# Two-layer hybrid encoder on one core: cast order in the down product, one reordered tile, postponed reciprocals, a last product in token halves

## Chip, cores and metric

One core of one Trainium2 chip runs the whole kernel in one launch. The metric is device time in microseconds (us), from the first to the last instruction with what lies around them; lower is better.

## The reference, cut to what matters

Input and output are 1024 tokens by 1024 channels in float32, and there are two layers. Layer 0 mixes tokens with a gated MLP over blocks of 128 tokens; layer 1 is attention over chunks of 64 tokens, each of which sees itself and the 8 chunks before it, with 16 heads of 64 channels and a clipped relative-position bias. Both layers end in a gated feed-forward block with a causal convolution of width 3, and a final RMSNorm closes.

```python
def conv_ffn(h, w_in, conv_w, conv_b, w_down):      # D_FF = 2816
    a = h @ w_in
    ...  # depthwise causal convolution of width 3, plus conv_b
    up, gate = jnp.split(a, 2, axis=-1)
    return (jax.nn.silu(gate) * up) @ w_down

# layer 0
h = h + gmlp_mixer(rmsnorm(h, a_norm_g[0]), ...)
h = h + conv_ffn(rmsnorm(h, f_norm_g[0]), ...)
# layer 1: keys and values come from the residual stream once
kv = rmsnorm(h, kv_norm_g) @ w_kv
h = h + chunk_attention(rmsnorm(h, b_norm_g[0]), k, v, ...)
h = h + conv_ffn(rmsnorm(h, f_norm_g[1]), ...)
return rmsnorm(h, final_norm_g)
```

## The kernel before

The residual stream h lies transposed, as 8 tiles of 128 channels by 1024 tokens; the two halves of 512 tokens are called t = 0 and t = 1. A float32 product is made of three matmuls in a faster format: each operand is split into a high part, the cast of itself by ScalarE, and a low part, the subtraction of that cast by VectorE (`split`, L135 to L138). High times high, low times high and high times low go into one PSUM bank.

**Order of the work.** TensorE's instructions run in the order in which the program writes them. On the other engines and queues a planner sets the order at build time from its own estimate of when an instruction's inputs are ready; each engine then runs its list strictly in order. `tc.issue_after(ins)` keeps what is issued inside it behind `ins` if both are on the same engine. `put_off(us, fn)` issues `fn` once the matmuls issued since add up to so many us of the program's own clock, so it also sets where `fn`'s matmuls stand in TensorE's list.

**Feed-forward, up side** (`ffn`, L636). Up and gate are computed by a Strassen scheme in 7 products, numbered 1 to 7, per tile of 128 of the 2816 features (`NF` = 22 tiles). A product is 12 matmuls of 512 columns. Products share PSUM: product 6 leaves a sum in one half of the gate bank, ScalarE copies it out (`keep`, L693), and product 7 goes on accumulating in that same half; product 3 goes on in the half where product 5 left its own. Tiles 0 and 1 are computed plainly, tile 2 is the first with 7 products, and the list `steps` (L658) writes the order out. After product 3 come the convolution of the up part, after product 4 that of the gate part and then SiLU (`conv`, `gated`). POOL makes the sums of blocks for the next stage and SyncE's queue stores them.

**Feed-forward, down side** (`down`, L779). Again 7 products, in the order 1, 6, 2, 7, 5, 4, 3, each over 11 steps: 77 steps a layer. A step takes a block d and a block g, splits them into w and x, and feeds 12 matmuls (3 for each of 4 output tiles m). Loads bring two steps at once (a set: one d tile and one g tile); sets take turns in two pools, two sets of every four from `new_raw`, two from `dx`. The w tiles have 4 places, the x tiles 16 that they share with others. `make` (L803) prepares steps up to four ahead. Up to step 23 the order on ScalarE, VectorE and SyncE is the program's own (`entry`); from step 24 on it is the planner's. When a product's 11 steps are done, `whole` (L815) adds its bank to h: product 7 adds into two tiles of h for each m, on POOL. In layer 1 the last four steps are taken together, output tile by output tile, so that the first tiles can be finished while the last are computed. When a half of the tokens is complete, `rstd_rows` sums the squares over channels by matmuls against ones (L229) and the norm follows (`norm` in layer 0, `final` in layer 1).

**Attention.** Heads go in pairs, each head in 8 blocks of keys. TensorE interleaves scores, values, the maxima of the next head (`Max`, L1054 and L1061, read by VectorE at L1057 and L1063), and the projections of the next pair. At the end of each half of the tokens a pair divides its outputs: `piece` (L1161) takes the reciprocal of the denominators in four pieces and multiplies; the fourth splits the result and stores it (`osave`). `stage` (L945) copies a head's keys and queries into place by DMA.

## Time and profile before

| | before |
|---|---|
| median of 3 runs | 2217.21 us (2214.3 to 2220.84) |
| the profiled execution | 2217.12 us |
| its span, first to last instruction | 2215.3 us |
| mean granted TensorE clock | 0.993 |
| TensorE matmul busy | 2152.2 us |

The times of the rows below are from that one profiled execution, counted from the start of its span. The mean granted clock is 1 at 2.4 GHz and 0.5 at 1.2 GHz.

### The profile page before, as it was taken

How to read it: one execution, taken by the hardware profiler on the slowest of the kernel's cores; microseconds unless marked ns; L12 is line 12 of the kernel's file. 1: busy time of each engine (PE TensorE's matmuls, PEld its weight loads, DVE VectorE, ACT ScalarE, POOL GpSimd, SP SyncE). 2: the span in 40 equal slices, each digit the busy share in tenths (PEclk: the TensorE clock that was granted, in tenths of full speed). 3: DMA queues.
4: the chain of work that ended last, by engine and by line, in shares of the span. 5: the costliest groups of instructions: out<-in, count | busy, mean ns of one | idle time of the engine just before them, and what ended most of it. 6: DMA issues, size and time to landing. Idle time of an engine off the chain costs nothing.

```text
span 2215.3 us, 28221 instructions
## 1 busy us (share of the span) xinstructions
PE 2152.2 (97%) x9880; PEld 1781.0 (80%) x9880; DVE 1584.9 (72%) x2418; ACT 1083.0 (49%) x1909; POOL 686.0 (31%) x471
## 2 busy tenths in 40 slices
PE   8999999999999999999999999999999999999998
PEld 7888887888888887768888888777778888888876
DVE  4763878988888665565776776654988888885555
ACT  6544445445444543445555555552544444454433
POOL 0301314423334112044444444351343334241020
PEclk9999999999999999999999999999999999999999
DMA  5242233445445865435444444644244444477652
GB/s 205 86 141 78 86 105 137 164 143 174 147 165 200 306 216 191 166 110 124 124 108 117 110 119 124 185 164 156 76 171 161 158 157 164 140 245 284 216 182 105
DMA packets 151534, 344.04 MB, mean 155 GB/s; under 512 B 31840, under 2 KB 32224, under 8 KB 151392
## 3 DMA queue, kind: packets, MB, share of 16 engines
q1 hardware_dynamic: 148080, 336.26, 46.7%
q10 hardware_dynamic: 3312, 5.98, 0.7%
q8 instruction: 77, 1.26, 0.2%
q14 instruction: 65, 0.53, 0.1%
HBM read 225.20 MB, written 87.56 MB: 141 GB/s over the span
## 4 chain that ended last, share of the span: by engine, by line
PE 48%; DVE 20%; issue 13%; DMA 11%; ACT 4%; POOL 2%; SPq 1%; POOLq 0%; DVEq 0%; ACTq 0%
DVE wlo L138 6%; DMA raw<-gT 5%; PE vps L465 4%; PE up L354 4%; PE up L356 4%; PE up L359 4%; PE gate L354 3%; PE gate L356 3%; PE gate L359 3%; DMA raw<-in_f_win 3%; DVE yl L138 2%; PE qkv L186 2%; PE qkv L182 2%; PE qkv L179 2%; DVE a L704 2%
## 5 line engine op out<-in xcount | busy, mean ns | idle before, releaser
L138 DVE TENSOR_TENSOR wlo<-raw,whi 128x512 fp32r<-128x512 f32 x425 | 365.8, 876 | 160.1 <-ACT whi L137 160.1
L137 ACT CAST whi<-raw 128x512 fp32r<-128x512 f32 x429 | 263.1, 626 | 206.3 <-PE gate L853 87.1
L354 PE MATMUL up<-yh,whi 128*128 128x512 f32 x688 | 269.4, 392 | 2.8 <-ACT gate L757 2.7
L356 PE MATMUL up<-yh,wlo 128*128 128x512 f32 x688 | 268.4, 390 | 0.0
L1114 POOL TENSOR_TENSOR pl<-p,ph 128x640 fp32r<-128x640 f32 (+4 forms) x128 | 163.9, 1283 | 197.1 <-ACT ph L1113 123.5
L138 DVE TENSOR_TENSOR yl<-raw,yh 128x512 fp32r<-128x512 f32 x180 | 130.4, 751 | 112.4 <-ACT yh L137 112.3
L354 PE MATMUL gate<-th,whi 128*128 128x512 f32 x496 | 194.6, 392 | 5.5 <-ACT h L695 5.5
L356 PE MATMUL gate<-th,wlo 128*128 128x512 f32 x496 | 194.5, 392 | 0.0
L718 POOL TENSOR_TENSOR h<-a 128x512 f32<-128x512 f32 x44 | 75.4, 1714 | 367.5 <-DVE a L710 350.3
L359 PE MATMUL up<-yl,whi 128*128 128x512 f32 x688 | 184.0, 389 | 0.0
L137 ACT CAST yh<-raw 128x512 fp32r<-128x512 f32 x184 | 107.8, 617 | 139.8 <-DMA raw<-gT 105.6
L354 PEld LDWEIGHTS up<-yh,whi 128*128 128x128 f32 x688 | 129.4, 188 | 34.2 <-ACT gate L757 7.5
L359 PEld LDWEIGHTS up<-yl,whi 128*128 128x128 f32 x688 | 129.2, 188 | 26.9
L356 PEld LDWEIGHTS up<-yh,wlo 128*128 128x128 f32 x688 | 129.4, 188 | 26.4
L182 PE MATMUL qkv<-yh,wlo 128*128 128x512 f32 x336 | 134.3, 400 | 0.0
L359 PE MATMUL gate<-tl,whi 128*128 128x512 f32 x496 | 133.5, 391 | 0.0
L137 ACT CAST whi<-S 128x512 fp32r<-128x512 f32 x160 | 99.1, 619 | 68.4 <-PE up L359 61.7
L179 PE MATMUL qkv<-yh,whi 128*128 128x512 f32 x336 | 132.5, 394 | 0.0
L853 PE MATMUL up<-yh,wlo 128*128 128x512 f32 x308 | 122.1, 396 | 10.1 <-DVE wlo L138 10.1
L369 POOL TENSOR_TENSOR h<-h 128x512 f32<-128x512 f32 x44 | 80.5, 1844 | 140.9 <-DMA h<-in_f_wdown 116.4
L853 PE MATMUL up<-yh,whi 128*128 128x512 f32 x308 | 120.8, 392 | 0.9 <-ACT whi L137 0.9
L853 PE MATMUL up<-yl,whi 128*128 128x512 f32 x308 | 121.2, 394 | 0.0
(252 smaller groups left out, 5322.4 us busy)
## 6 DMA issues: line engine op xcount, KB each, us to landing
raw<-in_f_win SPq DMA_DIRECT2D x88, 512.0 KB, 3.8
gT<-h SPq DMA_DIRECT2D x88, 256.0 KB, 4.2
h<-in_f_wdown SPq DMA_DIRECT2D x44, 512.0 KB, 5.1
dS<-h SPq DMA_DIRECT2D x88, 256.0 KB, 2.0
raw<-dS SPq DMA_DIRECT2D x40, 512.0 KB, 4.1
raw<-gT SPq DMA_DIRECT2D x40, 512.0 KB, 6.0
gB<-a SPq DMA_DIRECT2D x66, 256.0 KB, 2.3
raw<-in_f_wdown SPq DMA_DIRECT2D x30, 512.0 KB, 3.9
```

Source lines behind the costliest of these rows:

```text
L137: S.copy(hi, src)
L138: return eng.tensor_tensor(lo, src, f32(hi), op=ALU.subtract)
L179: nc.tensor.matmul(ps, wh[:, k, :], xs[k][0], start=k == 0, stop=False)
L182: nc.tensor.matmul(ps, wl[:, k, :], xs[k][0], start=False, stop=False)
L354: nc.tensor.matmul(ps, wh[:, k, :], xs[k][0], start=first and k == 0, stop=False, skip_group_check=True)
L356: nc.tensor.matmul(ps, wl[:, k, :], xs[k][0], start=False, stop=False, skip_group_check=True)
L359: nc.tensor.matmul(ps, wh[:, k, :], xs[k][1], start=False, stop=k == 3, skip_group_check=True)
L369: eng.tensor_tensor(A[n], a, b, op=op)
L465: nc.tensor.matmul(ps, a, b, start=k == i == 0, stop=k == KD - 1 and i == 2)
L718: G.tensor_tensor(B[n], x, B.get(y) if isinstance(y, str) else y, op=ALU.subtract)
L853: nc.tensor.matmul(ps, w[:, ms], x, start=q == i == 0 and p in (1, 6, 5, 4), stop=q == NP - 1 and i == 2, skip_group_check=True)
L1114: marks[2] = G.tensor_tensor(pl[:, :n], pf[:, :n], f32(ph[:, :n]), op=ALU.subtract)
```

## The change

- In `down`, each step's cast and subtraction of w, then of x, are kept behind those of the step before, on ScalarE and on VectorE (`order`).
- In `ffn`, tile 2 takes product 3 ahead of product 7.
- In attention, the reciprocals of the second token half are issued 20 us after the half is complete and not 0.5 us, for all pairs but the last two.
- The last four steps of layer 1's down product are done first for tokens 512 to 767 and then for 768 to 1023, with matmuls of 256 columns. The first quarter's final norm is issued while the second is computed. Each quarter's row sums also take in squares that were not added up by VectorE before.
- From the 21st set of loads on, `dx` and `new_raw` change places; the last step of layer 1 gets w tiles of its own; two `put_off` of 6.0 become 8.5, ahead of the row sums of the first token half (`norm`, `final`).

```diff
@@ -134,7 +134,7 @@
 
     def split(hi, lo, src, eng=V):
 
-        S.copy(hi, src)
+        behind[S] = S.copy(hi, src)
         return eng.tensor_tensor(lo, src, f32(hi), op=ALU.subtract)
 
     class Halves:
@@ -209,26 +209,34 @@
 
     accs = [2]
 
-    def square_sum(acc, h, m, pool):
+    def square_sum(acc, h, m, pool, cs=slice(0, H), apart=False):
 
         if m < 2:
             acc.append(pool.tile([P, H], F32, tag="acc", name="acc", bufs=accs[0]))
             S.activation(acc[m], h, AF.Square)
             return
         sq = pool.tile([P, H], F32, tag="f", name="sq")
+        sq = sq[:, cs]
         S.activation(sq, h, AF.Square)
-        a = acc[0 if m == KD - 1 else m % 2]
+        if m == KD - 1 and apart:
+            acc.append(sq)
+            return
+        a = acc[0 if m == KD - 1 else m % 2][:, cs]
         (G if m == 2 else V).tensor_tensor(a, a, sq, op=ALU.add)
-        if m == KD - 2:
-            V.tensor_tensor(a, a, acc[1], op=ALU.add)
-
-    def rstd_rows(acc, pool, then):
+        if m == KD - 2 and not (apart and cs.start):
+            V.tensor_tensor(a, a, acc[1][:, cs], op=ALU.add)
+
+    def rstd_rows(acc, pool, then, cs=slice(0, H)):
 
         pt = psS("pm")
-        for i in range(4):
-            nc.tensor.matmul(pt[:, i:i + 1], acc[0][:, i * P:(i + 1) * P], ones[:, 0:1], start=True, stop=True)
-            tick(0)
-        then(rstd_of(pt[:, :4], 4, pool))
+        sums = [acc[0][:, cs], *([acc[1][:, cs]] if len(acc) > 2 and cs.start else []), *acc[2:]]
+        n = (cs.stop - cs.start) // P
+        for k, a in enumerate(sums):
+            for i in range(n):
+                nc.tensor.matmul(pt[:, i:i + 1], a[:, i * P:(i + 1) * P], ones[:, 0:1], start=k == i == 0,
+                                 stop=k == len(sums) - 1, skip_group_check=True)
+                tick(0)
+        then(rstd_of(pt[:, :n], n, pool))
 
     def new_y():
         return yp.tile([P, H], F32R, tag="yh", name="yh"), yp.tile([P, H], F32R, tag="yl", name="yl")
@@ -269,7 +277,7 @@
                 ys[t][k] = norm_tile(h[k][:, halves[t]], bc, k, gain, npl)
             for k in range(KD):
                 put_off(0.9 * k, lambda k=k: tile_k(k))
-        put_off(8.5 if t else 6.0, lambda: rstd_rows(acc, npl, lambda r: put_off(2.9 if t else 6.0, lambda: scale(r))))
+        put_off(8.5, lambda: rstd_rows(acc, npl, lambda r: put_off(2.9 if t else 6.0, lambda: scale(r))))
 
 
 
@@ -658,7 +666,7 @@
                  (1, "A21", "B12"), (1, "A21", "B11"), (1, "A22", "B22"), (2, 1, None), (1, "A22", "B21")]
         plain = len(steps)
         shared = {6: 4, 7: 5, 13: 12, 16: 14}
-        steps += [(2, p, None) for p in (2, 5, 6, 7, 3)]
+        steps += [(2, p, None) for p in (2, 5, 6, 3, 7)]
         for j in range(3, NF):
             steps += [(j - (p == 4), p, None) for p in (1, 4, 5, 6, 2, 7, 3)]
         steps.append((NF - 1, 4, None))
@@ -789,7 +797,7 @@
 
             def load(p, q):
                 n = min(2, NP - q)
-                g, d = (dx.tile([P, 2, H], F32, tag="raw", name="raw") if sets[0] % 4 >= 2 else new_raw([P, 2, H])
+                g, d = (dx.tile([P, 2, H], F32, tag="raw", name="raw") if (sets[0] % 4 >= 2) != (sets[0] >= 20) else new_raw([P, 2, H])
                         for _ in range(2))
                 sets[0] += 1
                 src = {1: wd[:, q:q + n, 0, halves[0]], 2: wd[:, q:q + n, 1, halves[0]],
@@ -805,14 +813,21 @@
                 if (p, q) not in raw:
                     load(p, q)
                 d, g = raw.pop((p, q))
-                w, x = new_w(), new_y()
-                split(*w, d)
-                split(*x, g)
+                w, x = None, new_y()
+                if l and len(ready) == len(steps) - 1:
+                    w = tuple(du.tile([P, H], F32R, tag=n, name=n, bufs=1) for n in ("wlh", "wll"))
+                w = w or new_w()
+                for parts, src in ((w, d), (x, g)):
+                    with tc.issue_after(order[S].ins) if order else ExitStack(), \
+                            tc.issue_after(order[V].ins) if order else ExitStack():
+                        order[V] = split(*parts, src)
+                    order[S] = behind[S]
                 ready.append((w, x))
 
+            order = {}
             s1, acc = [None] * 4, [[], []]
 
-            def whole(p, m, ps):
+            def whole(p, m, ps, cs=slice(0, H), sums=None):
 
                 (h11, h12), (h21, h22) = ([h[i][:, hs] for hs in halves] for i in (m, m + 4))
                 if p == 1:
@@ -826,8 +841,9 @@
                         G.tensor_tensor(x, x, u, op=ALU.add)
                     return
                 x, t, k = {2: (h11, 0, m), 5: (h22, 1, m), 4: (h21, 0, m + 4), 3: (h12, 1, m + 4)}[p]
-                V.tensor_tensor(x, ps, x, op=ALU.add)
-                square_sum(acc[t], x, k, npl)
+                x = x[:, cs]
+                behind["h"] = V.tensor_tensor(x, ps[:, cs], x, op=ALU.add)
+                square_sum(sums or acc[t], x, k, npl, cs, bool(sums))
 
             accs[0] = 4
             bank = {b: [psum[n][i][:, hs] for hs in halves for n in ("up", "gate")] for i, b in enumerate("ab")}
@@ -843,25 +859,31 @@
                 b = "a" if p in (1, 2, 5, 3) else "b"
                 if n > len(steps) - end:
                     continue
-                todo = range(n, n + end if n == len(steps) - end else n + 1)
-                for m in range(4):
+
+                def tiles(m, todo, cs=slice(0, H)):
                     ps, ms = bank[b][m], slice(m * P, (m + 1) * P)
                     for k in todo:
                         q = steps[k][1]
                         (wh, wl), (xh, xl) = ready[k]
                         for i, (w, x) in enumerate(((wh, xh), (wl, xh), (wh, xl))):
-                            nc.tensor.matmul(ps, w[:, ms], x, start=q == i == 0 and p in (1, 6, 5, 4),
+                            nc.tensor.matmul(ps[:, cs], w[:, ms], x[:, cs], start=q == i == 0 and p in (1, 6, 5, 4),
                                              stop=q == NP - 1 and i == 2, skip_group_check=True)
-                            tick()
-                    if q == NP - 1 and len(todo) > 1:
-                        whole(p, m, ps)
-                for k in todo:
-                    ready[k] = True
+                            tick(cs.stop - cs.start)
+                    return ps
+                if n == len(steps) - end and l:
+                    for cs in (slice(0, H // 2), slice(H // 2, H)):
+                        sums = list(acc[1])
+                        for m in range(4):
+                            whole(p, m, tiles(m, range(n, n + end), cs), cs, sums)
+                        after(1, sums, cs)
+                    continue
+                for m in range(4):
+                    tiles(m, [n])
+                ready[n] = True
                 if q < NP - 1:
                     continue
-                if len(todo) == 1:
-                    for m in range(4):
-                        whole(p, m, bank[b][m])
+                for m in range(4):
+                    whole(p, m, bank[b][m])
                 if p == 4:
                     del psum["banks"]
                     psum["turn"].close()
@@ -1169,7 +1191,7 @@
                             nc.sync.dma_start(osave[0, p, :, halves[t]], f32(oh))
                             nc.sync.dma_start(osave[1, p, :, halves[t]], f32(ol))
                 for i in range(4):
-                    put_off(0 if p == LAST else (0.5 if t else 5.0) + 2.0 * i, lambda i=i: piece(i))
+                    put_off(0 if p == LAST else (5.0 if t == 0 else 20.0 if p < LAST - 1 else 0.5) + 2.0 * i, lambda i=i: piece(i))
 
         for t in range(2):
             first("v", t)
@@ -1321,15 +1343,17 @@
 
     gained = []
 
-    def final(n, acc):
+    def final(n, acc, cs=slice(0, H)):
         if not fg:
             for j in range(2):
                 fg.append(yp.tile([P, H], F32, tag="yl", name="fg"))
                 nc.scalar.dma_start(fg[j], fgain[halves[j]].partition_broadcast(P))
+        i0, blocks = cs.start // P, range(cs.start // P, cs.stop // P)
 
         def rows(r, i, j):
             ps, o = back(n, i, j), new_o()
-            V.scalar_tensor_tensor(o, ps, r[:, i:i + 1], fg[j], op0=ALU.mult, op1=ALU.mult)
+            with tc.issue_after(behind["h"].ins):
+                V.scalar_tensor_tensor(o, ps, r[:, i - i0:i - i0 + 1], fg[j], op0=ALU.mult, op1=ALU.mult)
             store(n, i, j, o)
 
         def gain(i):
@@ -1338,15 +1362,15 @@
             gained.append(new_o())
             V.tensor_tensor(gained[i], ps, fg[1], op=ALU.mult)
 
-        def last(r):
-            for i in range(4):
-                S.mul(gained[i], gained[i], r[:, i:i + 1])
-                store(1, i, 1, gained[i], nc.scalar)
-                rows(r, i, 0)
+        def scaled(r):
+            for i in blocks:
+                S.mul(gained[i], gained[i], r[:, i - i0:i - i0 + 1])
+                store(1, i, 1, gained[i], nc.scalar if i0 else nc.sync)
+                put_off(4.0, lambda i=i: rows(r, i, 0))
         if n:
-            put_off(1.6, lambda: rstd_rows(acc, npl, last))
+            put_off(1.6 if i0 else 2.6, lambda: rstd_rows(acc, npl, scaled, cs))
         else:
-            put_off(6.0, lambda: rstd_rows(acc, npl, lambda r: [
+            put_off(8.5, lambda: rstd_rows(acc, npl, lambda r: [
                 put_off(2.9 + 0.6 * i, lambda i=i: rows(r, i // 2, i % 2)) for i in range(8)]))
             for i in range(4):
                 put_off(16.0 + 0.8 * i, lambda i=i: gain(i))
```

## Rows read from the trace of the kernel before

**Rows 1.** The page: busy time, share of the span and instructions of each engine.
```profile
PE 2152.2 (97%) x9880; PEld 1781.0 (80%) x9880; DVE 1584.9 (72%) x2418; ACT 1083.0 (49%) x1909; POOL 686.0 (31%) x471
```

**Rows 2.** TensorE's waits, whole span: total us, times, longest us.
```profile
PE up L853 <- DVE wlo L138: 10.1, 6, 2.7
...
PE gate L354 <- ACT h L695: 5.5, 4, 2.1
...
PE pm L229 <- DVE acc L221: 4.6, 3, 2.3
...
PE qk L179 <- ACT whi L137: 2.3, 1, 2.3
...
PE qk L182 <- DVE wlo L138: 1.3, 1, 1.3
```

**Rows 3.** A stretch of layer 0's down product: busy us by engine, granted clock, DMA.
```profile
868.50:878.00 9.50, 7.67 (x27) 6.19 (x28) 6.90 (x9) 1.66 (x3) 7.54 (x5) 0.82 0.64 221
```

**Rows 4.** Timeline of ScalarE in layer 0's down product, in `entry` and behind it.
```profile
790.35 0.62 ACT L137 CAST whi<-raw 128x512 fp32r<-128x512 f32 x1 [1.58 <-PE gate L853]
...
841.28 1.14 ACT L137 CAST yh<-raw 128x512 fp32r<-128x512 f32 x2 [5.11 <-DMA raw<-gT]
```

**Rows 5.** A stretch that holds most of `entry` in layer 0, columns as in rows 3.
```profile
700.00:800.00 100.00, 100.00 (x443) 82.86 (x442) 67.66 (x87) 50.82 (x84) 23.68 (x16) 1.00 0.77 275
```

**Rows 6.** DMA issues of the down product: KB each, median us from issue to landing.
```profile
raw<-gT SPq DMA_DIRECT2D x40, 512.0 KB, 6.0
```

**Rows 7.** Timeline of VectorE and POOL behind product 7, layer 0.
```profile
863.40 12.65 POOL L826 TENSOR_TENSOR h<-h,u 128x512 f32<-128x512 f32 x8 [32.10 <-DVE u L824]
...
865.13 3.48 DVE L138 TENSOR_TENSOR yl<-raw,yh 128x512 fp32r<-128x512 f32 x2
```

**Rows 8.** Timeline of TensorE behind product 7, both layers.
```profile
865.26 0.50 PE L853 MATMUL up<-yh,wlo 128*128 128x512 f32 x1 [2.04 <-DVE wlo L138]
...
2112.98 0.80 PE L853 MATMUL up<-yh,wlo 128*128 128x512 f32 x1 [2.25 <-DVE wlo L138]
```

**Rows 9.** Timeline of ScalarE and VectorE at tile 2 of layer 0.
```profile
357.64 0.57 ACT L695 COPY h<-gate 128x512 f32<-128x512 f32 x1
...
371.21 1.58 DVE L369 TENSOR_TENSOR S<-raw 128x512 f32<-128x512 f32 x1 [2.33 <-DMA raw<-in_f_win]
```

**Rows 10.** TensorE's waits from 1055 to 1376, across the ends of attention's first six pairs.
```profile
PE mx L1061 <- DVE mb L1057: 3.9, 7, 0.8
PE mx L1054 <- DVE mb L1057: 3.8, 4, 1.2
```

**Rows 11.** The reciprocals (ns min/median/max), and a stretch 20 us behind a pair's end.
```profile
L1164 DVE RECIPROCAL den<-den x64: 894/939/954, 1060.9 to 1477.4; 128x128 f32<-128x128 f32 x64
...
1154.00:1158.00 4.00, 4.00 (x21) 3.50 (x20) 0.42 (x1) 1.26 (x4) 0.79 (x2) 1.00 0.87 179
```

**Rows 12.** Timeline of SyncE's queue and TensorE at the second head of the seventh pair.
```profile
1395.40 0.33 SPq L996 DMA_DIRECT2D yh<-osave  x1
1395.83 0.47 SPq L954 DMA_DIRECT2D km<-thi  x1
...
1400.02 0.30 PE L1054 MATMUL mx<-km,qe 128*128 128x128 f32 x1 [1.52 <-DMA km<-thi]
```

**Rows 13.** Timeline of SyncE's queue, start of the first projections of layer 1.
```profile
953.76 0.33 SPq L154 DMA_DIRECT2D raw<-in_w_q  x1
```

**Rows 14.** Timeline of TensorE and VectorE at the end of the kernel.
```profile
2201.30 0.39 PE L853 MATMUL gate<-yl,whi 128*128 128x512 f32 x1
2204.01 1.02 PE L229 MATMUL pm<-ones,acc 128*128 128x1 f32 x8 [2.32 <-DVE acc L221]
...
2206.41 2.83 DVE L1332 SCALAR_TENSOR_TENSOR o<-fin,st,fg 128x512 f32<-128x512 f32 x4 [1.18 <-POOL st L198]
```

**Rows 15.** Timeline of TensorE, matmuls of 256 columns in attention.
```profile
1158.15 0.28 PE L1132 MATMUL po<-ph,vl 128*128 128x256 f32 x1
1158.27 0.28 PE L1134 MATMUL po<-pl,vh 128*128 128x256 f32 x1
```

## Prediction

> **What bounds the kernel now.** I read the page first. The reader is to see TensorE at 97% of the span and VectorE, the next one, at 72% [rows 1]: the kernel is bound by TensorE's list of matmuls, and an edit can only win where that list stands still or runs at the lower clock. So I listed next whom TensorE waits for [rows 2], and then cut the span into short stretches to see the granted clock. A 512-column matmul takes a place of 100/443 = 0.226 us when nothing is missing [rows 5]. Span less TensorE's busy time is 2215.3 - 2152.2 = 63 us [rows 1], and the waits are grouped: the down product waits for the subtraction `wlo`, tile 2 of the up side waits for the copy in `keep`, attention waits for the maxima, and the row sums wait for VectorE. Longer waits cost twice: after some waits of 2 us or more the granted clock falls for a while to the lower level, 1.2 GHz. In one stretch it is 0.82 over 9.5 us [rows 3], so 9.5 x 0.18 = 1.7 us are lost besides the wait. There are five such stretches where the change works: two in down (behind product 7 in each layer), one at tile 2 in each layer, one at the start of layer 1's projections. I take 1.7 us for each.
>
> **Down casts in step order: 12.5 us won.** Nothing is added but an order. `wlo` holds TensorE up for 10.1 us in 6 waits [rows 2], all of them behind step 24, where the planner sets the order, and two slow stretches follow: 10.1 + 2 x 1.7 = 13.5 us. Rows 4 show how it comes about. In `entry` ScalarE casts w, then x, and waits only for TensorE to free a w place. Behind it the planner puts casts of x (`yh`), for steps further on, ahead of w casts: at 841.28 ScalarE stood 5.1 us for x data not yet landed, and the w cast behind it came late, and with it the freeing of the load places that the next transfer needs. `entry` runs the order that the change asks for, with the same places and the same transfers: in the 100 us of rows 5 TensorE's busy time is 100.00 us. A step is 12 x 0.226 = 2.7 us, and in that order w can be ready up to three steps ahead of use: 8 us, which cover a cast and a subtraction. What is queued behind a w cast that waits for TensorE is the step's own x cast, and the squares and stores of h; none is due within a step. I leave 1.0 us for product 7's end, where VectorE shares with POOL. Bounds: 3.7 us (rival one) and 13.5. The swap of `dx` and `new_raw` makes four sets in a row use `dx`, so two sets start their load only when the ones two before are cast, some 8 us ahead of need against a landing of 6.0 us [rows 6]; I cost it at nothing, hidden by those three steps, and at one landing a layer if they are not there.
>
> **Product 3 ahead of product 7: 4.5 us won.** `keep` waits behind a SiLU on ScalarE and reads at 357.64 what product 7 must go on with [rows 9]. TensorE's waits on it are 5.5 us in 4, the longest 2.1 [rows 2]: 2.1 in each layer at tile 2, the other 1.3 at tile 3. Product 3 needs nothing of that copy and fills 2.7 us, more than the wait. Both waits and both slow stretches go: 2 x (2.1 + 1.7) = 7.6 us. But VectorE is late next: at 371.21 it stands 2.33 us for a load that its queue, not TensorE, delays [rows 9], and TensorE would come 3.8 us earlier to the same subtractions. If that wait stays, most of it comes back at tile 3. Bounds 0 and 7.6; I take 4.5, above the middle, since the convolution of the up part now starts a product earlier and can fill that idle time.
>
> **Reciprocals put off: 4.5 us won.** Around the ends of the first six pairs TensorE waits 3.9 + 3.8 = 7.7 us for the maxima [rows 10]. Four reciprocals of 0.94 us and their products stand there in VectorE's list [rows 11]. 20 us later VectorE is busy 0.42 us of 4 [rows 11], so the wait itself should go. What moves too are the two `osave` stores on SyncE's queue: by the program's clock the fourth piece ends some 27 us behind the pair's end, close to where `stage` copies `km` for the next head. In the seventh pair one 256 KB transfer right ahead of that copy cost TensorE 1.52 us [rows 12]. Six such hits would be 9.1 us. Bounds: 7.7 - 9.1 = -1.4, and 7.7. I take two hits in six, 7.7 - 3.0, rounded down.
>
> **Entry of layer 1, and the later row sums: 4.5 + 2 us won.** The first weights of the projections are loaded at 953.76 [rows 13], when the last set leaves `new_raw`; they pass POOL, ScalarE and VectorE and make TensorE wait 2.3 + 1.3 us [rows 2], with a slow stretch: 5.3 us. After the swap the last two sets lie in `dx`, so `new_raw` is free three steps earlier, some 8 us, which is more than the 3.6 us missing. I leave 0.8 us for the second half's norm, which TensorE then reaches earlier; bounds 0 and 5.3. The row sums wait 4.6 us in 3 [rows 2], of which 2.3 is at the very end [rows 14]; for the other 2.3 the later place (2.5 us) is enough. I take 2.0; bounds 0 and 2.3.
>
> **Last steps in token halves: 3 us won.** The last matmul ends at 2201.7 and the span at 2215.3 [rows 14]: 13.6 us of tail. Added: 96 matmuls of 256 columns, 0.12 us apart [rows 15], for 48 of 512: 11.5 - 10.8 = 0.7 us lost. Won: the 2.32 us up to the row sums [rows 14] are an addition, a square and a sum over 512 columns; half as wide and without the sum it is about half, 1.2 us. Of four final products, 2.83 us, two are left at the end: 1.4 us. Half of the last eight stores start earlier; the others still have to land, so I take 1.1 us. Together 1.2 + 1.4 + 1.1 - 0.7 = 3.0; bounds 1 (the landing of the last store hides the rest) and 5.
>
> **The sum.** 12.5 + 4.5 + 4.5 + 4.5 + 2.0 + 3.0 = 31.0 us. The profiled execution took 2217.12 us, 1.8 of it around its span, 0.1 under the median of the runs. 2217.1 - 31.0 = 2186.1, so 2186 us.
>
> **Rivals.** One: the waits behind product 7 are contention and not order. POOL adds for 12.65 us there, and two of VectorE's subtractions take 3.48 us [rows 7], where four instructions of their size take 2.83 elsewhere [rows 14]. Three waits lie there, from 2.04 to 2.25 us [rows 8]: 6.4 us, and with both slow stretches 9.8. If they stay, the order wins 13.5 - 9.8 = 3.7, and if VectorE sets tile 2 as well, that edit wins 1: 31.0 - 8.8 - 3.5 = 18.7 us, or 2198. For it speaks that POOL's work is unchanged; against it that with w three steps ahead the four stretched steps need some 3 us of 8. The Trainium skill (SBUF — State Buffer, section SBUF: two separate sides) says that VectorE with two operands in SBUF and POOL take turns at one pair of ports, whole instructions at a time; the slow subtractions of rows 7 agree, and by that rule no order of casts takes the contention away. That is this rival's time.
>
> Two: `osave` hits the `km` copy in each pair. The edit then loses 1.4: 31.0 - 5.9 = 25.1 us, or 2192. For it: the two fall within about 1 us. Against: the queue's order is the planner's, and it may put the copy first.
>
> Three, the other side: down becomes bound by its loads. x is no longer cast ahead, and a place is freed only when w and x of its step are cast. If just one set were under way, a release, a landing of 6.0 us [rows 6] and two casts of 0.62 [rows 4] and two subtractions of 0.7 (2.6 us) would make 8.6 us a set, for 5.4 of matmuls: 3.2 us on each of some 52 sets behind step 24, 166 us. The order then wins nothing and the other parts 18.5: 2217.1 - 18.5 + 166 = 2365 us. It decides from (18.5 + 6.7)/52 = 0.5 us a set. Against it: rows 5, in the same order. For it: the four sets in a row in one pool. The Trainium skill (TensorE: Matmul & The Clock Gate, the table at its head) calls ScalarE's and VectorE's queues strictly first in, first out, 8 deep; by that rule a w cast that waits for TensorE holds the x casts behind it, and only rows 5 say that this costs nothing.
>
> Four: the waits only move. VectorE and the loads set the pace, TensorE meets them a step later, and only 0 to 6 us remain: about 2214.
>
> **Chances.** The forecast has 0.60, rival one 0.17, two 0.10, three 0.06, four 0.07. About 0.3%, 6.7 us, is what a measurement can tell from no change. Faster is the forecast with one and two, 0.87; the same is four, 0.07; slower is three, 0.06. All terms at their upper bounds win 13.5 + 7.6 + 7.7 + 5.3 + 2.3 + 5 = 41.4 us, or 2175.7, so the range starts at 2175. Upward it takes in rivals one and two with the weaker bounds of one more part, the entry and the row sums (2198.4 + 6.5 = 2204.9): to 2205. Three, four and what one and two leave above it are out.
>
> **What would show it.** Order: no wait of L853 for `wlo` over 0.5 us, in ScalarE's list w and x casts in turn to the end of down. Product 3: no wait on L695 at tile 2, clock 1 there; if wrong, the wait stands at tile 3 or in front of product 2. Reciprocals: no wait on L1057 at the pair ends; if wrong, waits on `km` some 32 us behind them. Entry: `in_w_q` issued by 945 or so, no wait in front of the first projection. Tail: last matmul to end under 10.5 us. The forecast is wrong if the planner, which sees a changed program everywhere, makes new waits where nothing was edited, or if rows 5 do not carry over to the steps behind 24.

## The result, and the profile after

The changed kernel takes 2184.81 us (median of 4 runs, 2182.97 to 2188.74) against 2216.27 us before on the same chip: a ratio of 0.9858, 95% interval 0.9836 to 0.9879, so 31.5 us less (27 to 36). 2186 us had been predicted. The profiled execution took 2183.77 us, with a span of 2182.0 us.

The page of the changed kernel, section 1, as in [rows 1] (busy us, share of the span, instructions):

```profile
PE 2139.9 (98%) x9940; PEld 1778.9 (82%) x9940; DVE 1590.5 (73%) x2425; ACT 1083.0 (50%) x1913; POOL 685.7 (31%) x472
```

TensorE's busy time fell by 12.3 us with 60 more matmuls in the list; the other 21.0 us of the 33.3 that the span lost were idle time, which is now 2182.0 - 2139.9 = 42.1 us. Part of the fall in busy time is the granted clock, 0.996 on the mean for 0.993: 2182 x 0.003 = 6.5 us.

TensorE's waits in the changed kernel, whole span, as in [rows 2] (total us, times, longest us). L869 is the down matmul now, L703 the copy in `keep`, L1076 and L1083 the products of `Max`, L1128 the addition in `score`, L236 the row-sum product:

```profile
PE gate L362 <- ACT h L703: 4.8, 2, 2.4
PE mx L1076 <- DVE p L1128: 4.6, 5, 1.0
PE st L1122 <- DMA qe<-mr: 3.9, 2, 3.7
PE mx L1076 <- DMA ks<-tlo: 3.0, 1, 3.0
...
PE pm L236 <- DVE acc L225: 1.3, 1, 1.3
```

No line of L869 is left: the down product, 10.1 + 0.9 us before, waits for nothing. The copy of `keep` costs nearly what it did (4.8 for 5.5), in two waits and not four. The maxima wait for another VectorE instruction than before. Both row-sum waits inside down are gone; one of 1.3 us stands behind layer 0's down product.

Lengths of the stages in us, each the difference of two starts in TensorE's timeline of the profiled execution (a down stage runs from its first matmul to its last, "entry" from there to attention's first maximum, "attention" on to its last value product, "tail" from the last down matmul of layer 1 to the end of the span). The last column is the median of the timed runs; the rows below the second are the experiments of the next section (e9 is the changed kernel traced a second time):

| kernel | up 0 | down 0 | entry | attention | up 1 | down 1 | tail | median |
|---|---|---|---|---|---|---|---|---|
| before | 433.2 | 224.5 | 48.9 | 466.7 | 435.2 | 221.7 | 14.0 | 2216.27 |
| changed | 432.5 | 211.0 | 44.8 | 464.2 | 432.7 | 217.1 | 9.3 | 2184.81 |
| e1 order alone | 435.4 | 215.0 | 45.9 | 465.5 | 433.7 | 219.6 | 13.7 | 2202.71 |
| e10 order and row sums | 434.9 | 211.1 | 49.6 | 467.1 | 435.4 | 215.5 | 14.5 | 2198.29 |
| e2 no order | 432.5 | 218.7 | 43.9 | 464.5 | 432.8 | 228.2 | 9.3 | 2198.65 |
| e5 old row sums | 433.0 | 220.3 | 43.3 | 462.6 | 432.7 | 221.1 | 9.3 | 2194.40 |
| e11 old sets | 433.1 | 211.1 | 48.9 | 463.8 | 432.0 | 217.0 | 9.3 | 2189.15 |
| e3 old tile 2 | 434.0 | 211.1 | 44.7 | 464.4 | 434.3 | 217.1 | 9.3 | 2185.63 |
| e4 old reciprocals | 433.7 | 211.1 | 44.7 | 467.2 | 432.9 | 217.0 | 9.5 | 2187.04 |
| e6 one part | 433.6 | 211.1 | 44.7 | 464.8 | 432.0 | 215.6 | 13.0 | 2186.38 |
| e7 S1 behind | 430.8 | 211.1 | 44.7 | 465.3 | 430.8 | 217.0 | 9.3 | 2181.56 |
| e8 denser pieces | 432.2 | 211.0 | 44.7 | 464.8 | 434.0 | 217.0 | 9.4 | 2185.94 |
| e9 changed again | 433.0 | 211.1 | 44.9 | 462.9 | 432.4 | 217.0 | 9.3 | 2184.81 |
| e12 both more | 430.9 | 211.0 | 44.8 | 461.8 | 430.7 | 217.0 | 9.3 | 2179.08 |

A stage that an edit does not touch repeats within 0.2 us in down 0 and tail, within 2 in the up stages and within 2.7 in attention (462.6 to 465.3 in the kernels with the changed reciprocals), so a difference of 2 or 3 us in one of the last three is not shown by these lengths alone. The profiled execution is also not always a typical one: those of e2, e10 and e3 are the slowest of their kernels (5.6, 3.7 and 2.2 us over the median), and e12's is the fastest (2.8 under it). The gain sits in down 0 (13.5 us), down 1 and tail (9.3), entry (4.1), attention and up 1 (2.5 each).

Windows behind product 7 and the timeline of ScalarE in the changed kernel's layer 0, to set beside [rows 3, 4]:

```profile
852.00:872.00 20.00, 20.00 (x89) 16.54 (x89) 17.95 (x19) 8.49 (x15) 12.74 (x8) 1.00 0.49 158
```

```profile
837.75 0.62 ACT L137 CAST whi<-raw 128x512 fp32r<-128x512 f32 x1 [1.58 <-PE gate L869]
838.28 0.61 ACT L137 CAST yh<-raw 128x512 fp32r<-128x512 f32 x1
840.47 0.62 ACT L137 CAST whi<-raw 128x512 fp32r<-128x512 f32 x1 [1.58 <-PE gate L869]
841.00 0.61 ACT L137 CAST yh<-raw 128x512 fp32r<-128x512 f32 x1
```

ScalarE now casts w and x in turn and waits only for TensorE to free a place. TensorE is busy for all 20.00 us at full clock, although POOL is about as busy as before (12.74 us, 12.65 in [rows 7]).

The end of the changed kernel, timeline of TensorE and VectorE, which answers to [rows 14]: last down matmul 2172.67, span 2182.0, so 9.3 us of tail for 14.0:

```profile
2172.67 0.28 PE L869 MATMUL gate<-yl,wlh 128*128 128x256 f32 x1
2173.67 0.95 PE L236 MATMUL pm<-ones,acc 128*128 128x1 f32 x8
...
2176.14 1.41 DVE L1356 SCALAR_TENSOR_TENSOR o<-fin,st,fg 128x512 f32<-128x512 f32 x2 [0.88 <-POOL st L198]
```

### The profile page after: what moved, and what is told of

Its sections match the earlier page's. It is cut to its first block, busy times and chain, and to the rows that moved or that the text cites. A ratio compares the mean times of both kernels' runs of the same rounds, so it can differ in the third digit from the quotient of the medians.

```text
span 2182.0 us, 28383 instructions
## 1 busy us (share of the span) xinstructions
PE 2139.9 (98%) x9940; PEld 1778.9 (82%) x9940; DVE 1590.5 (73%) x2425; ACT 1083.0 (50%) x1913; POOL 685.7 (31%) x472
## 4 chain that ended last, share of the span: by engine, by line
PE 69%; DVE 16%; issue 5%; DMA 5%; ACT 3%; POOL 1%; SPq 0%; DVEq 0%; POOLq 0%; ACTq 0%
PE gate L869 9%; PE up L869 9%; DVE wlo L138 6%; PE vps L473 4%; PE up L362 4%; PE up L364 4%; PE up L367 4%; PE qkv L182 3%; DMA raw<-in_f_win 3%; PE qkv L179 3%; PE qkv L186 3%; PE gate L362 3%; PE gate L364 3%; PE gate L367 3%; DVE a L712 3%
## 5 line engine op out<-in xcount | busy, mean ns | idle before, releaser
L138 DVE TENSOR_TENSOR wlo<-raw,whi 128x512 fp32r<-128x512 f32 (+1 forms) x424 | 369.6, 881 | 228.2 <-ACT whi L137 228.1
L137 ACT CAST whi<-raw 128x512 fp32r<-128x512 f32 (+1 forms) x428 | 266.5, 628 | 330.3 <-PE gate L869 200.7
L362 PE MATMUL up<-yh,whi 128*128 128x512 f32 x688 | 269.2, 391 | 0.9 <-ACT gate L765 0.6
L364 PE MATMUL up<-yh,wlo 128*128 128x512 f32 x688 | 268.0, 390 | 0.0
L367 PE MATMUL up<-yl,whi 128*128 128x512 f32 x688 | 183.9, 389 | 0.0
L138 DVE TENSOR_TENSOR yl<-raw,yh 128x512 fp32r<-128x512 f32 x180 | 145.3, 811 | 8.9 <-ACT yh L137 8.8
L869 PE MATMUL up<-yl,whi 128*128 128x512 f32 (+1 forms) x312 | 120.6, 387 | 0.0
L869 PE MATMUL up<-yh,whi 128*128 128x512 f32 (+1 forms) x312 | 120.4, 386 | 0.0
L869 PE MATMUL gate<-yh,wlo 128*128 128x512 f32 (+1 forms) x312 | 120.4, 386 | 0.0
L869 PE MATMUL up<-yh,wlo 128*128 128x512 f32 (+1 forms) x312 | 120.3, 386 | 0.0
```

What stands on the lines that cost most here:

```text
L137: behind[S] = S.copy(hi, src)
L138: return eng.tensor_tensor(lo, src, f32(hi), op=ALU.subtract)
L362: nc.tensor.matmul(ps, wh[:, k, :], xs[k][0], start=first and k == 0, stop=False, skip_group_check=True)
L364: nc.tensor.matmul(ps, wl[:, k, :], xs[k][0], start=False, stop=False, skip_group_check=True)
L367: nc.tensor.matmul(ps, wh[:, k, :], xs[k][1], start=False, stop=k == 3, skip_group_check=True)
L869: nc.tensor.matmul(ps[:, cs], w[:, ms], x[:, cs], start=q == i == 0 and p in (1, 6, 5, 4), stop=q == NP - 1 and i == 2, skip_group_check=True)
```

## The experiments

Each ratio is to the kernel before on the same chip, with its 95% interval; a difference from the changed kernel is one of medians, against 2184.81, and is known to some 3 us.

### The order of the casts: done alone (e1), and undone (e2)

The kernel before with this edit only; e2 takes the same lines back out of the changed kernel.

```diff
-                split(*w, d)
-                split(*x, g)
+                for parts, src in ((w, d), (x, g)):
+                    with tc.issue_after(order[S].ins) if order else ExitStack(), \
+                            tc.issue_after(order[V].ins) if order else ExitStack():
+                        order[V] = split(*parts, src)
+                    order[S] = behind[S]
```

> The kernel before with one edit of the change alone: in the down projection the casts (ScalarE) and the subtractions (VectorE) of the steps keep the order of the steps. Theory of the order: the waits on wlo at the down matmul (10.1 us in all before) and the one long slow-clock stretch of layer 0 go, and the time falls by 13 to 18 us, to about 2200, with the down projection of layer 0 shorter by 12 to 14 and that of layer 1 by 3 to 5. Rival, contention of VectorE and POOL behind the seventh product: that part of the wait stays, and the time falls by 3 to 6 us only.

> The changed kernel with the order of the down casts and subtractions left to the scheduler again. Theory of the order: the waits on wlo at the down matmul come back, and the kernel is 13 to 18 us slower than the changed one, about 2200. Rival, that the other edits had already moved the late casts away: the down projection of layer 0 stays within 4 us of the changed kernel's.

e1: 2202.71 us, ratio 0.9930 (0.9914 to 0.9947), 15.7 us less than before; down 0 is 9.5 us shorter and not 12 to 14, down 1 2.1 and not 3 to 5. e2: 2198.65 us, ratio 0.9910 (0.9888 to 0.9933), 13.8 us more than the changed kernel. All waits on `wlo` at the down matmul go with the order and 9.2 us of them come back without it, so contention of VectorE and POOL behind product 7 alone does not make TensorE wait; what it adds to the waits under the old order was not separated. But e1's down 0 is 4.0 us longer than the changed kernel's. Timeline of TensorE and a window behind it in e1 (columns as in [rows 3]):

```profile
923.68 1.05 PE L229 MATMUL pm<-ones,acc 128*128 128x1 f32 x8 [2.17 <-DVE acc L221]
...
2155.54 1.05 PE L229 MATMUL pm<-ones,acc 128*128 128x1 f32 x8 [2.17 <-DVE acc L221]
```

```profile
922.00:932.00 10.00, 8.32 (x34) 6.88 (x35) 4.10 (x8) 2.13 (x4) 1.02 (x1) 0.83 0.00 1
```

With the order in, TensorE comes earlier to the row sums of the first token half and waits 2.17 us for VectorE's sum in each layer (1.6 and 0.7 in the trace of before), and the granted clock falls to 0.83 over the 10 us behind it: 2.17 + 10 x 0.17 = 3.9 us, which is what e1's down 0 has too much.

### Row sums and load sets (e5, e10, e11)

e5 undoes the later row sums in the changed kernel; e10 puts order and later row sums, and nothing else, into the kernel before; e11 undoes the turn of the load buffers in the changed kernel.

```diff
-        put_off(8.5, lambda: rstd_rows(acc, npl, lambda r: put_off(2.9 if t else 6.0, lambda: scale(r))))
+        put_off(8.5 if t else 6.0, lambda: rstd_rows(acc, npl, lambda r: put_off(2.9 if t else 6.0, lambda: scale(r))))
...
-            put_off(8.5, lambda: rstd_rows(acc, npl, lambda r: [
+            put_off(6.0, lambda: rstd_rows(acc, npl, lambda r: [
```

```diff
-                g, d = (dx.tile([P, 2, H], F32, tag="raw", name="raw") if (sets[0] % 4 >= 2) != (sets[0] >= 20) else new_raw([P, 2, H])
+                g, d = (dx.tile([P, 2, H], F32, tag="raw", name="raw") if sets[0] % 4 >= 2 else new_raw([P, 2, H])
```

> The changed kernel with one edit undone: the matrix products that add up the row sums of the first token half are again due 6.0 instead of 8.5 us behind the half's last square. Theory read from the run with the order alone, where this product still waited 2.17 us for VectorE's sum once in each down projection and the clock then fell to 0.91 for 20 us: both waits come back, the down projection of layer 0 is 4 us longer and that of layer 1 3 us, the kernel 6 to 8 us slower than the changed one. Rival, that the edit is worth the 2.0 us of the prediction's sum: 1 to 3 us slower.

> The kernel before with two edits of the change alone: the order of the down casts and subtractions, and the row-sum products of the first token half due 8.5 instead of 6.0 us behind the last square. Theory that these two are worth most of the 31 us together, because without the later row sums the two waits of 2.17 us and their slow-clock stretches take part of the order's gain back: 8 to 10 us faster than the order alone, about 2193, with no wait of TensorE in the down projection but at its end, and the down projection of layer 0 at 211 us. Rival, that the row sums are worth the 2.0 us of the prediction: about 2200.

> The changed kernel with the buffers of the last down loads taken in the old turn. Prediction's term for the entry of layer 1 was 4.5 us (0 to 5.3). Theory read from the run with the order alone, where the first projection followed the last down matmul in 0.3 us without this edit, and one wait of 2.3 us for wlo stood behind it: 1 to 3 us slower than the changed kernel. By the prediction's term it would be 4 to 5 us slower.

e5: 2194.40 us, ratio 0.9906 (0.9889 to 0.9923), 9.6 us slower than the changed kernel; down 0 is 9.3 us longer, more than expected, and down 1 4.0. In e5's down 0 the wait is again 2.17 us, waits of 2.7 us in all for `yl` and `yh` begin 25 us later, and the granted clock is 0.54 and 0.77 in two stretches of 5 us behind the first:

```profile
920.00:925.00 5.00, 4.49 (x15) 3.92 (x16) 1.30 (x3) 0.00 (x0) 1.02 (x1) 0.54 0.53 210
925.00:930.00 5.00, 5.00 (x19) 4.02 (x18) 1.29 (x2) 1.70 (x4) 0.00 (x0) 0.77 0.00 2
```

That makes 2.2 + 2.7 + 5 x 0.46 + 5 x 0.23 = 8.4 of the 9.3 us. e10: 2198.29 us, ratio 0.9922 (0.9908 to 0.9936): next to e1 only 2 us by the ratios, 4.4 by the medians, nearer to the rival. Yet its down stages are 3.9 and 4.1 us shorter than e1's, as the theory said; the entry is 3.7 us longer. Timeline of TensorE and a window at the entry in e10:

```profile
949.00 0.80 PE L179 MATMUL qk<-yh,whi 128*128 128x512 f32 x1 [2.20 <-ACT whi L137]
```

```profile
946.00:956.00 10.00, 6.84 (x18) 4.77 (x17) 8.76 (x13) 5.58 (x9) 6.46 (x3) 0.66 0.46 164
```

Nearly half of what the row sums gave, the entry took: TensorE is there before the first weights. e11, with both of those edits and without the turn of the buffers, is 2189.15 us, ratio 0.9878 (0.9863 to 0.9894), 4.3 us slower, the price of the prediction's term and not the 1 to 3 of this run's own theory, and has the same two waits there (2.20 and 1.26 us). SyncE's queue in e10 and then in the changed kernel, first load of the projections' weights (953.76 before, [rows 13]):

```profile
938.09 0.33 SPq L154 DMA_DIRECT2D raw<-in_w_q  x1
```

```profile
919.04 0.33 SPq L154 DMA_DIRECT2D raw<-in_w_q  x1
```

With the turn of the buffers the load goes out 19 us earlier, 15 of them against the end of down, and the first projection follows the last down matmul in 0.3 us where it took 2.6. So with the order in, the later row sums show their full worth only when the buffers are turned too. The turn without the row sums was not run by itself; in e5, which has it and all other edits, the entry is 43.3 us for e1's 45.9.

### Product 3 ahead of product 7 (e3, e7)

e3 puts the old order back into the changed kernel; e7 keeps the new one and moves a block sum in VectorE's list.

```diff
-        steps += [(2, p, None) for p in (2, 5, 6, 3, 7)]
+        steps += [(2, p, None) for p in (2, 5, 6, 7, 3)]
```

```diff
-            src = block_sum(...)
+            with tc.issue_after(behind["conv", 1].ins) if p == 5 and j == 4 else ExitStack(): src = block_sum(...)
...
-                V.scalar_tensor_tensor(a[:, d:], src[:, :T - d], ...
+                behind["conv", part] = V.scalar_tensor_tensor(a[:, d:], src[:, :T - d], ...
```

> The changed kernel with the products of the third d_ff tile in their old order (2, 5, 6, 7, 3). Theory that the edit is worth what the tables by stage show, 0.7 us in the first half of layer 0 and 2.5 us in that of layer 1: 2 to 4 us slower than the changed kernel, the 5.5 us of waits on the convolution's ScalarE copy back at tile 2 and the two waits of 2.4 us at tile 3 gone. Rival, that the waits of tile 3 come from the load of the fifth tile and not from this order: both stand, the waits at tile 2 are back and those of 2.4 us stay, and it is 5 to 8 us slower.

> The changed kernel with one edit more: in VectorE's list the block sum S1 of the fifth d_ff tile (it waits 3.24 us for its load) stands behind the third tile's gate convolution and no longer in front of it. Theory that this wait holds up the convolution, the SiLU, the ScalarE copy and so TensorE: the waits of 2.40 and 2.42 us at the fourth tile fall under 0.7 each, the slow-clock stretch of layer 1 behind the second goes, and the kernel is 4 to 6.5 us faster than the changed one. Rival, that the copy is late for another reason (ScalarE's own list): the waits stay over 1.5 us and the time is the changed kernel's.

e3: 2185.63 us, ratio 0.9853 (0.9838 to 0.9868): 0.8 us slower by the medians, 3.1 us by the two up stages (1.5 and 1.6), which is hardly outside what up stages vary by untouched. Both waits stand in it, 2.12 us at tile 2 and 2.16 at tile 3, the second hardly smaller than the changed kernel's 2.40. So the waits are those that the rival named, and the price is the smaller one: (2.12 + 2.16) - (0.60 + 2.40) = 1.3 us a layer. That is steadier than the lengths: from the first matmul of the up stage to the one at tile 3 that waits for the copy are 80.0 to 80.1 us in both layers of every traced kernel with the old order (before, e1, e10, e3) and 78.8 in all eight that have the new one without e7's edit. The edit is worth some 1.2 us a layer at that point. The same matmul in the kernel before, at 379.85, and in e1:

```profile
379.85 0.50 PE L354 MATMUL gate<-th,whi 128*128 128x512 f32 x1 [0.67 <-ACT h L695]
```

```profile
380.10 0.50 PE L354 MATMUL gate<-th,whi 128*128 128x512 f32 x1 [2.15 <-ACT h L695]
```

Before, the granted clock was 0.66 in the 5 us behind the wait at tile 2 and the wait at tile 3 is short; in e1 the clock stayed at 1.00 there and the wait is 1.5 us longer. A window of before:

```profile
358.00:363.00 5.00, 4.74 (x14) 3.75 (x15) 4.53 (x7) 1.86 (x5) 4.54 (x1) 0.66 0.01 3
```

Both reach tile 3 some 80 us after the start of their stage (299.8 and 300.1), so the slow stretch at tile 2 cost almost nothing: TensorE would have waited for the same copy. Why the second wait stays is read in the changed kernel's timeline at tile 3:

```profile
370.86 1.01 DVE L377 TENSOR_TENSOR S<-raw 128x512 f32<-128x512 f32 x1 [3.24 <-DMA raw<-in_f_win]
...
376.15 1.06 ACT L717 ACTIVATE a<-a 128x1024 f32<-128x1024 f32 x1 [5.16 <-DVE a L712]
377.12 0.57 ACT L703 COPY h<-gate 128x512 f32<-128x512 f32 x1
...
377.74 0.50 PE L362 MATMUL gate<-th,whi 128*128 128x512 f32 x1 [2.40 <-ACT h L703]
```

The block sum S1 of tile 4 waits for its load at the head of VectorE's list, the gate convolution stands behind it, the SiLU behind that, then the copy, then TensorE. e7 moves S1 alone: 2181.56 us, ratio 0.9843 (0.9828 to 0.9858), 3.3 us faster than the changed kernel, up stages 1.7 and 1.9 us shorter. Timeline of ScalarE in e7, where the SiLU comes 2.4 us earlier, though the stage began 1.3 us later:

```profile
373.74 1.06 ACT L717 ACTIVATE a<-a 128x1024 f32<-128x1024 f32 x1 [1.44 <-DVE a L712]
374.71 0.57 ACT L703 COPY h<-gate 128x512 f32<-128x512 f32 x1
```

TensorE's waits in e7 from 1523 to 1955 (layer 1's up side):

```profile
PE up L362 <- ACT gate L765: 1.5, 2, 1.2
PE gate L362 <- DVE gate L779: 0.6, 1, 0.6
```

No wait on the copy is left. Some 1 us a layer comes back elsewhere (1.2 in the longest wait here), and e7 falls short of the 4 to 6.5 expected by less than medians can tell.

### The reciprocals (e4, e8)

e4 puts the old times back, e8 sets the moved pieces closer together.

```diff
-                    put_off(0 if p == LAST else (5.0 if t == 0 else 20.0 if p < LAST - 1 else 0.5) + 2.0 * i, lambda i=i: piece(i))
+                    put_off(0 if p == LAST else (0.5 if t else 5.0) + 2.0 * i, lambda i=i: piece(i))
```

```diff
-                    put_off(0 if p == LAST else (5.0 if t == 0 else 20.0 if p < LAST - 1 else 0.5) + 2.0 * i, lambda i=i: piece(i))
+                    put_off(0 if p == LAST else (5.0 if t == 0 else 20.0 if p < LAST - 1 else 0.5) + (1.0 if t and p < LAST - 1 else 2.0) * i, lambda i=i: piece(i))
```

> The changed kernel with attention's reciprocals put off by the old times (0.5 and 5 us). Theory of the reciprocals: the waits at the ends of the pairs come back (3.9 and 3.8 us in all), those of 0.9 us behind the moved piece and the two DMA waits of the seventh pair fall back to 1.5 and 2.6 us, so that it is 1.5 to 4 us slower than the changed kernel. Rival, that the moved pieces cost as much as they free: within 1 us.

> The changed kernel with the four moved reciprocal pieces of a pair 1.0 instead of 2.0 us apart, so that they end 3 us earlier (they start as before, 20 us behind the pair). Theory that the five waits of 0.9 us (4.6 us in all) at the first maximum of each second head come from the last piece and its split in front of the score's addition on VectorE, and the seventh pair's DMA wait from osave in front of its copies: the five waits fall to under 1.5 us in all, the seventh pair's wait of 2.95 us falls by 1 us or more, attention is 3 to 6 us shorter. Rival, that denser pieces hold up the scores: new waits on the additions appear inside the pair, and attention is not shorter by 1 us.

e4: 2187.04 us, ratio 0.9855 (0.9841 to 0.9870): 2.2 us slower by the medians, attention 3.0 us longer. Its waits from 1030 to 1450, whose last two of the seventh pair are 1.6 and 3.0 (3.0 and 3.7 in the changed kernel):

```profile
PE mx L1076 <- DVE mb L1079: 6.4, 6, 1.7
PE mx L1083 <- DVE mb L1079: 3.3, 7, 0.8
PE st L1122 <- DMA qe<-mr: 3.0, 1, 3.0
PE mx L1076 <- DMA km<-thi: 1.6, 1, 1.6
```

Of these 9.7 us the first wait, 1.68 us at 1030.06, is in the changed kernel too (1.62 us at 1029.59, just ahead of 1030). So 8.0 us of waits go with the edit, and in their place come 4.6 us (five of 0.9) and 2.1 us more at the seventh pair: 8.0 - 4.6 - 2.1 = 1.3 us by the waits. The length of a pair says more. From one of the products for a maximum to the same product in the next pair, at a granted clock of 1.00, e4 takes 58.99 us and the changed kernel 58.12:

```profile
1118.17 0.38 PE L1076 MATMUL mx<-km,qe 128*128 128x256 f32 x1 [1.15 <-DVE mb L1079]
1177.16 0.39 PE L1076 MATMUL mx<-km,qe 128*128 128x256 f32 x1 [0.91 <-DVE mb L1079]
```

```profile
1141.29 0.30 PE L1076 MATMUL mx<-km,qe 128*128 128x128 f32 x1 [0.89 <-DVE p L1128]
1199.41 0.30 PE L1076 MATMUL mx<-km,qe 128*128 128x128 f32 x1 [1.00 <-DVE p L1128]
```

Over four pairs in a row e4 takes 59.0 to 59.3 and both traces of the changed kernel 58.0 to 58.2. That is 1 us in each of five pairs, less the 2.1 at the seventh: some 3 us, which agrees with the stage's length. Why a pair is 1 us shorter, when its listed waits fall by half of that, was not shown. Where the five come from stands in the changed kernel's timeline of VectorE and TensorE:

```profile
1137.37 1.65 DVE L138 TENSOR_TENSOR ol<-o,oh 128x512 fp32r<-128x512 f32 x1 [0.46 <-ACT oh L137]
1138.94 0.41 DVE L1128 TENSOR_TENSOR p<-st,bias 128x256 f32<-128x256 f32 x1
...
1141.29 0.30 PE L1076 MATMUL mx<-km,qe 128*128 128x128 f32 x1 [0.89 <-DVE p L1128]
```

The split of the moved pieces stands in front of the score's addition. e8 brings it 3 us forward: 2185.94 us, ratio 0.9861 (0.9844 to 0.9877), not faster. The five waits are gone and five others have come, since two reciprocals and not one now stand ahead of the row maximum's last step (1.75 us at 1128.76, then L1087 at 1130.43). TensorE's waits in e8, 1030 to 1356:

```profile
PE mr L1092 <- DVE mb L1087: 4.1, 5, 0.8
PE mx L1076 <- DVE mb L1079: 1.5, 1, 1.5
```

### The last steps in one part (e6)

```diff
-                    for cs in (slice(0, H // 2), slice(H // 2, H)):
+                    for cs in (slice(0, H),):
```

The row sums of this one part are due 1.6 us behind it, and its stores use the queue of the second half.

> The changed kernel with the last four down steps done once for all 512 tokens and not for two groups of 256. Theory of the token halves: what stands behind the last matmul grows from 9.3 us to 13 or 14, less 0.7 us of slower 256-column matmuls, so that it is 3 to 4.5 us slower than the changed kernel. Rival, that the tail got shorter by the rows that were put off and not by the halves: within 1 us.

2186.38 us, ratio 0.9866 (0.9852 to 0.9881): 1.6 us slower by the medians. The tail is 13.0 us for 9.3 and down 1 is 215.6 for 217.1, so the halves win 3.7 - 1.5 = 2.2 us in the profiles, less than the 3 expected. The cost is twice the 0.7 us counted: the first half's row-sum products (0.50 and 0.58 us busy, from 2169.05 to 2169.99 in the changed kernel) now stand in front of the last down matmul.

### The changed kernel again, and a faster one (e9, e12)

e12 is the changed kernel with the edit of e7, and with the pieces of e8 due from 21.0 us on and not from 20.0, so that no second one stands ahead of the row maximum's last step. (The first still does, as in the changed kernel; the text below puts it behind, which is not what the trace shows.)

> The changed kernel itself once more, as the mark for the three kernels beside it: 0.984 to 0.988 of the kernel before, about 2185.

> The changed kernel with two edits more: the fifth d_ff tile's block sum S1 behind the third tile's gate convolution on VectorE (3 us faster by its own run), and the moved reciprocal pieces 1.0 us apart from 21 us on, so that the first stands behind the row maximum's last step and not in front of it (there the denser pieces from 20 us on put six waits of 0.8 us in place of five of 0.9). Theory that those waits were the order of three VectorE instructions and no more: neither the waits at the first maximum nor those at the row maximum are left over 1.5 us in all, attention is 2 to 5 us shorter than the changed kernel's, and with S1 it is 5 to 9 us faster than the changed kernel. Rival, that any place of the pieces holds up something of the same size: 2 to 4 us faster, by S1 alone.

e9: 2184.81 us, ratio 0.9860 (0.9842 to 0.9877). e12: 2179.08 us, ratio 0.9833 (0.9817 to 0.9849): 5.7 us under the changed kernel, 0.26%, with intervals that overlap a little; all four runs of e12 (2176.29 to 2180.77) lie under all four of e9 (2182.60 to 2185.95) on the same chip. The stages agree, up 0 and up 1 1.6 and 2.0 us shorter and attention 2.4. A pair takes 57.5 to 57.6 us for 58.0 to 58.2, at the same granted clock of 1.00:

```profile
1137.43 0.30 PE L1076 MATMUL mx<-km,qe 128*128 128x128 f32 x1 [0.43 <-DVE o L1174]
1194.92 0.30 PE L1076 MATMUL mx<-km,qe 128*128 128x128 f32 x1 [0.40 <-DVE o L1174]
```

TensorE's waits in e12, 1030 to 1356:

```profile
PE mx L1076 <- DVE o L1174: 2.0, 5, 0.4
```

Of five times 0.9 us five times 0.4 are left: more than the 1.5 us that the expectation allowed, but the larger part went with the order of a few VectorE instructions, as the theory said. The two DMA waits of the seventh pair (2.7 and 3.3 us) are still there; moving them was not tried.

## Why the prediction was right, and where its steps were not

The total was right within 1.2 us. The terms that it was added up from erred in both directions, so that closeness is in part luck: row sums were set too low, product 3 too high, and the cost of the reciprocals was sought in the wrong place. The term that carries the sum, the order, and the entry were right in mechanism and near in size.

**Order, 12.5 us.** Right in mechanism, and a little small: 15.7 us alone (11.8 to 19.1 by the interval), 13.8 when undone. The 1.0 us left for product 7 was not needed. Rival one was right about the contention and wrong about its price: in the changed kernel VectorE's subtractions there take 1.78 us where the same ones take 0.68 just behind, and TensorE does not wait:

```profile
863.51 1.78 DVE L138 TENSOR_TENSOR yl<-raw,yh 128x512 fp32r<-128x512 f32 x1
865.22 0.68 DVE L138 TENSOR_TENSOR wlo<-raw,whi 128x512 fp32r<-128x512 f32 x1
```

The Trainium skill (SBUF — State Buffer, section SBUF: two separate sides) gives the turn-taking at the ports that fits those 1.78 us; no more of it reaches the path. Down did not become load-bound (rival three): 211.0 us with the turned buffers and 211.1 without (e11), so that swap cost down nothing, as the prediction had put it.

**Row sums 2.0 and entry 4.5.** The entry measured 4.3 us (e11); the load goes out 15 us earlier against the end of down (e10 and the changed kernel), more than the 8 counted. The row sums were mis-sized: their bound of 2.3 us was read from the waits of before, which were short because TensorE came late. Once the order is in, they cost 8.0 us in the two down stages (e1 against e10). Of that, 3.7 us come back at the entry unless the weights are loaded earlier. The terms were added as if independent; undoing the row sums alone costs 9.6 us, adding them to the order alone gives 2 to 4.

**Product 3, 4.5 us.** Here a step failed: "above the middle, since the convolution of the up part now starts a product earlier and can fill that idle time". It filled some of it, but S1's wait grew from 2.33 to 3.24 us and the gate convolution stayed behind it. The sentence before that one, that the wait would come back at tile 3, is what happened. Its upper bound, 7.6 us, also counted two slow stretches as won, and e1 shows that at tile 2 a slow stretch is made up by a shorter wait at tile 3. The edit is worth 1.2 to 1.3 us a layer at tile 3, some 2.5 us in all, 3.1 by the stages and 0.8 by the medians; e7 shows the cause.

**Reciprocals, 4.5 us.** The waits at the pair ends went as predicted. The cost was sought in `osave` against `km` and found on VectorE, in front of the score; only the seventh pair shows a transfer that comes later (2.96 us for 1.52), and rival two's six hits did not occur. Worth some 3 us by the pairs and by attention's length, 2.2 by the medians, and not 4.5.

**Token halves, 3.0 us.** The tail fell to 9.3 us, under the 10.5 named. 2.2 us by e6's stages. The tail of e6 is itself 1.0 us shorter than before's: its row-sum product waits 0.23 us and not 2.32, because the last squares are no longer added up first (the products over these squares then wait another 0.26 us):

```profile
2173.21 1.02 PE L236 MATMUL pm<-ones,acc 128*128 128x1 f32 x8 [0.23 <-DVE acc L227]
```

Together 3.2 us for the 3.0 predicted, though a run with the squares alone was not made.

Taken out singly, the six parts cost 13.8 + 9.6 + 4.3 + 0.8 + 2.2 + 1.6 = 32.3 us by the medians, against 31.5 for the whole; each carries an uncertainty of some 3 us, as the intervals show, so the smaller three are known by their stages and waits only.

## What to carry to other kernels

A wait in the trace prices a cause only for the arrival time that the bound engine has now: when an earlier wait goes, the next one on the path grows, and its present length is not an upper bound. So list, for each wait removed, what the engine meets next, and change them together; here the row sums were worth about twice as much with the load buffers turned as without (9.6 us by e5, 4.4 by e10 against e1). Where an in-order engine idles, ask what stands at the head of its list: moving one block sum that waited for a load took away the wait that reordering the products around its effect had only moved. And, as at tile 2 here, a stretch at a slower clock costs nothing when the next wait on the path is shorter by as much.

## What the hardware showed that was not expected

The same wait did not always cost the clock. In the changed kernel the wait of 2.40 us at tile 3 leaves the granted clock at 1.00 in layer 0, and that of 2.42 us, in the same order of instructions, is followed by 0.74 and 0.92 in layer 1. In e9, the same kernel run again, it is the other way round, 0.66 behind the wait in layer 0 and 1.00 in layer 1. Windows of the changed kernel, then of e9:

```profile
375.00:380.00 5.00, 2.60 (x12) 1.89 (x11) 5.00 (x6) 2.57 (x4) 1.46 (x1) 1.00 0.21 85
380.00:385.00 5.00, 5.00 (x24) 4.14 (x23) 2.73 (x5) 1.73 (x3) 0.24 (x1) 1.00 0.64 218
1600.00:1605.00 5.00, 3.25 (x9) 2.58 (x10) 5.00 (x7) 2.57 (x4) 1.69 (x1) 0.74 0.16 55
1605.00:1610.00 5.00, 5.00 (x22) 4.10 (x21) 2.61 (x5) 1.73 (x3) 0.00 (x0) 0.92 0.84 297
```

```profile
380.00:385.00 5.00, 5.00 (x17) 3.92 (x16) 3.40 (x5) 1.35 (x3) 1.68 (x1) 0.66 0.39 120
1605.00:1610.00 5.00, 5.00 (x24) 4.14 (x23) 2.65 (x5) 1.73 (x3) 0.16 (x1) 1.00 0.64 219
```

In the eight traces that have this wait (2.39 to 2.43 us, once in each layer), the granted clock falls behind 12 of the 16.

So the 1.7 us that the prediction counted with each of five waits is paid only sometimes, and where it is paid a later wait can give it back: layer 1's up side is 432.7 us with the slow stretch and 432.4 in e9 without it. The kernel without the order (e2) also varied more over its four runs, 2192.44 to 2204.27 us, than any other kernel over four (at most 8.7 us); that the clock behind its waits is the reason was not shown.
